# A bidirectional chunked scan and an output projection on TensorE: the order of their matmuls written out by hand

## The chip, the core and the metric

The kernel runs on one core of a Trainium2 chip. The metric is the device time of one execution in microseconds (us), and less is better. TensorE (PE) multiplies matrices into PSUM; VectorE (DVE), ScalarE (ACT) and GpSimd (POOL) do the elementwise work; SyncE (SP) issues every DMA from one queue. The engines run side by side, and each works through its own list of instructions in order.

## The reference

One layer over 17 tiles of 128 tokens (16 of the latent, one of the context). A normalised input is projected to two groups of heads. Group A is a gated linear recurrence, group B a gated DeltaNet; each is scanned forward and backward. The outputs of both are normed per head, gated, joined and multiplied by `w_out`; a SwiGLU feed-forward network (FFN) follows.

```python
def step(s, inp):                 # gated delta rule, one chunk (group B)
    u_c, w_c, attn_c, q_c, kt_c, d_c = inp
    v_new = u_c - jnp.einsum('bhck,bhkv->bhcv', w_c, s)
    o_c = jnp.einsum('bhtk,bhkv->bhtv', q_c, s) + jnp.einsum('bhts,bhsv->bhtv', attn_c, v_new)
    s = s * d_c[..., None, None] + jnp.einsum('bhsk,bhsv->bhkv', kt_c, v_new)
    return s, o_c
...
o_b = ob_f + _flip(ob_b)
o_b = head_rms_norm(o_b, p['gdn_out_norm']) * jax.nn.silu(b_z)
y = jnp.concatenate([o_a, o_b], axis=-1) @ p['w_out']
x = x + g1 * y
h = rms_norm(x, p['norm2']) * (1 + sc2) + sh2
ff = (jax.nn.silu(h @ p['w_gate']) * (h @ p['w_up'])) @ p['w_down']
return x + g2 * ff
```

## The kernel before

The program has three parts: the input projection with group A's recurrence (to about 1297 us), the stage that is changed here (1297 to 1848 us), and the FFN. The stage holds three kinds of work on TensorE.

**The rest of the inverse.** `A3` turns the triangular systems of group B into inverses, one block for each of the 17 chunks, with some ten of them in this stage. A block is 56 float32 matmuls of 32 or 64 columns (lines 675, 681, 686, 696, 701) in a chain PE, ACT, PE, DVE, PE, ACT, PE, DVE, and its triangular solve (`A2`, lines 635 and 637) has run on POOL or DVE before. The last solve is that of the context tile.

**The scan.** `scan(d, c, pre)` does one chunk of one direction, in groups of four matmuls (one per head, float32, 128x128): `pkS` (line 927, keys times state), then four DVE operations that make `vn` (929), `pv` (933), an ACT copy `vv` (935), `pS` (938), four DVE operations that make the new state (943), `po` (947), `pa` (954). `scan_pre` of the next chunk gives `pqk` (905). The next chunk's `pkS` needs the new state. The loop takes 16 pairs: forward chunk i and backward chunk 15-i. From i = 8 on both chunks of a pair have been visited by the other direction, and their sum goes on to the projection.

**The output projection.** Per token tile and group (`part` 0 is A, `part` 1 is B, 34 items) `out_a` norms the heads on ACT, transposes them (`ot`, four matmuls, line 820), gates them and splits them into a high and a low part; `out_b` multiplies these by `w_out` in 24 matmuls of 128x512 (`py`, line 847), whose result DVE takes out of PSUM (851, 855) into a tile of the ring `xt5` of two; `out_c` norms five of the tiles for the FFN (`nt`, line 870). `load_wout` brings the eight row blocks of `w_out` through staging tiles `wor` of the same ring `xt5`. Blocks 0 to 3 are loaded ahead of the scan, 4 to 7 in pairs i = 0 to 3. The parts of blocks 4 to 7 lie in the pool `wb`.

Nothing of this order is written down: the framework's scheduler sorts the instructions of each engine by priority and a timing model when the program is built. The source has eight projection items ahead of the scan, then one or two per pair.

Of the kernel before, what the change touches and what calls it, by code (L numbers as in the profile page):

```python
# [15 lines left out]
P = 128  # L16
# [17 lines left out]
def hybrid_step(ctx: ExitStack, tc, x, vecs, ada1, ada2, bada, win, wgt, alog, dtb, sa, sb, wout, wg, wu, wd, normf,  # L34
# [755 lines left out]
    def out_a(c, part, ob):  # L790
# [35 lines left out]
    def out_b(c, part, oh, ol):  # L826

        xt = wk5.tile([P, D], F32, tag="xt5", name="xt5", bufs=2)
        gm = g1
        if part:  # L830
            x2 = wk5.tile([P, D], F32, tag="x2", name="x2", bufs=2)
            dma(out=xt, in_=xa_d[c])
            if c == NL:
                dma(out=x2, in_=x[LAT:TOK])
                gm = wk6.tile([P, D], F32, tag="h2", name="g1c")
                dma(out=gm, in_=mod_d[1:2, 0:D].broadcast_to([P, D]))
            else:
                for w in range(4):
                    dma(out=x2[32 * w:32 * w + 32], in_=rows_of(x, c, w))
        woh, wol = wos[part]  # L840
        for n in range(2):
            cs = slice(512 * n, 512 * n + 512)
            py = ps5.tile([P, 512], F32, tag="y", name="py", bufs=2)
            t = 0
            for k in range(H):
                for a, b in ((oh, woh), (oh, wol), (ol, woh)):
                    nc.tensor.matmul(out=py, lhsT=a[:, k], rhs=b[:, k, cs], start=t == 0,
                                     stop=t == 3 * H - 1)
                    t += 1
            if part:  # L850
                nc.vector.tensor_tensor(out=xt[:, cs], in0=py, in1=xt[:, cs], op=ALU.add)
                nc.gpsimd.tensor_tensor(out=xt[:, cs], in0=xt[:, cs], in1=gm[:, cs], op=ALU.mult)
                nc.gpsimd.tensor_tensor(out=x2[:, cs], in0=x2[:, cs], in1=xt[:, cs], op=ALU.add)
            else:
                nc.vector.tensor_copy(out=xt[:, cs], in_=py)
        if not part:
            dma(out=xa_d[c], in_=xt)
            return None
        dma(out=x2_d[c], in_=x2)
        return x2  # L860

    def norm_T(c, xt, h2, r, bank):

        nc.scalar.activation(out=xt, in_=xt, func=AF.Copy, scale=r)
        c2 = int(c == NL)
        for i in range(2):
            pt = bank()
            for j in range(H):
                k = H * i + j
                nc.tensor.transpose(pt[:, j], xt[:, k * P:(k + 1) * P], ident)  # L870
            for j in range(H):
                k = H * i + j
                nc.vector.tensor_scalar(out=h2[:, k], in0=pt[:, j], scalar1=m2[:, c2, KD + k:KD + k + 1],
                                        scalar2=m2[:, c2, k:k + 1], op0=ALU.mult, op1=ALU.add)
        dma(out=h2_d[c], in_=h2)

    def out_c(c, x2):
        if c in halves[0][:5]:
            norm_T(c, x2, wk6.tile([P, KD, P], F32, tag="h2", name="h2"), row_norm(x2, wk6),
                   lambda: psn.tile([P, H, P], F32, tag="nt", name="nt"))  # L880
# [16 lines left out]
    def scan_pre(d, c, kT, qT, kn, vn, e, X):  # L897
# [4 lines left out]
        pq = ps2.tile([P, H, P], F32, tag="pre", name="pqk", bufs=1)  # L902
        for h in range(H):
            nc.scalar.activation(out=e[:, h], in_=e[:, h], func=AF.Exp, bias=nG[:, d, c, h:h + 1])
            nc.tensor.matmul(out=pq[:, h], lhsT=kT[:, h], rhs=qT[:, h], start=True, stop=True)
        nc.vector.tensor_tensor(out=e, in0=pq, in1=e, op=ALU.mult)
# [3 lines left out]

    visited = set()
    last = [None]

    def scan(d, c, pre):
        kT, qT, kn, vn, at, X = pre
# [8 lines left out]
        if lat:  # L924
# [3 lines left out]
            for h in range(H):  # L928
                nc.vector.scalar_tensor_tensor(out=vn[:, h], in0=pk[:, h], scalar=nrg[:, d, c, h:h + 1],
                                               in1=vn[:, h], op0=ALU.mult, op1=ALU.add)  # L930
        pv = sc_("pv")
# [3 lines left out]
        nc.scalar.activation(out=vv, in_=pv, func=AF.Copy)  # L935
        pS = sc_("pS")
# [4 lines left out]
        if lat:  # L941
            for h in range(H):
                nc.vector.scalar_tensor_tensor(out=Sn[:, h], in0=So[:, h], scalar=eL[:, d, c, h:h + 1],
                                               in1=pS[:, h], op0=ALU.mult, op1=ALU.add)
            po = sc_("po")
# [6 lines left out]
        pa = sc_("pa")  # L952
        for h in range(H):
            last[0] = nc.tensor.matmul(out=pa[:, h], lhsT=at[:, h], rhs=vv[:, h], start=True, stop=True)
        second = c in visited
        visited.add(c)
        if second or not lat and d == 0:
            t = wk6.tile([P, H, P], F32, tag="ob", name="ob", bufs=3)
        else:
            t = W([P, H, P], "of", 2)  # L960
        if lat:
            for h in range(H):
                nc.scalar.activation(out=t[:, h], in_=po[:, h], func=AF.Copy, scale=eG[:, d, c, h:h + 1])
            nc.vector.tensor_tensor(out=t, in0=pa, in1=t, op=ALU.add)
        else:
            nc.scalar.activation(out=t, in_=pa, func=AF.Copy)
        if not second:
            if lat:
                dma(out=ob_d[c], in_=t)
                return None  # L970
            return t
        of = W([P, H, P], "or", 2)
        dma(out=of, in_=ob_d[c])
        nc.gpsimd.tensor_tensor(out=t, in0=t, in1=of, op=ALU.add)
        return t

    stage = []

    def out_step(item=None):

        stage.insert(0, item and (item[0], item[1], out_a(*item)))
        if len(stage) > 1 and stage[1]:
            c, part, a = stage[1]
            stage[1] = (c, part, out_b(c, part, *a))
        if len(stage) > 2:
            it = stage.pop()
            if it and it[1]:
                out_c(it[0], it[2])

    def scan_ctx():  # L990
        ts = []
        for d in range(2):
            a = scan_load(d, NL)
            scan_pre(d, NL, *a)
            ts.append(scan(d, NL, a))
            visited.discard(NL)
        nc.gpsimd.tensor_tensor(out=ts[0], in0=ts[0], in1=ts[1], op=ALU.add)
        return ts[0]
# [4 lines left out]
    todo = []  # L1003
    for _ in range(8):
        out_step(first.pop(0))
# [3 lines left out]
    pres = [scan_load(0, 0), scan_load(1, NL - 1)]  # L1009
    for d in range(2):  # L1010
        scan_pre(d, (0, NL - 1)[d], *pres[d])
    for i in range(NL):
        nxt = [scan_load(0, i + 1), scan_load(1, NL - 2 - i)] if i < NL - 1 else None
        for d, c in ((0, i), (1, NL - 1 - i)):
            o = scan(d, c, pres[d])
            if nxt:
                with tc.issue_after(getattr(last[0], "ins", last[0])):
                    scan_pre(d, (i + 1, NL - 2 - i)[d], *nxt[d])
            if o is not None:
                todo.append((c, 1, o))  # L1020
        pres = nxt
        if i < H:
            load_wout(H + i)
        if i == 2:
            todo.append((NL, 1, scan_ctx()))
        n = -(-len(first) // (8 - i)) if i < 8 else 2
        for _ in range(n):
            if first:
                out_step(first.pop(0))
# [530 lines left out]
```

## Time and profile before

| | us |
|---|---|
| median of 3 runs | 3359.61 (3348.92 to 3360.17) |
| the profiled execution | 3358.57 |
| its span, first to last instruction | 3356.9 |
| PE busy over the span | 3121.5 (93%) |
| last matmul of the input projection starts | 1297.4 |
| last `py` matmul starts | 1834.7 |
| first matmul of the FFN starts | 1848.4 |

The busy share over the span tells little here: the stage of interest is 551 us of it, and its stretches have different limits. The granted clock of TensorE has two levels, 1.2 and 2.4 GHz; a mean of 1.00 is full speed, and matmuls that take twice as long show the lower level. A float32 matmul leaves two instructions in the rows, so that a group of four is x8 there; a `py` matmul or a transpose leaves one. The rows further down are from this execution.

### The profile page before, as it was taken

The numbers are of one execution on the slowest core, as the hardware profiler recorded it, in microseconds if no ns is written. First come the engines' busy times: TensorE is split into PE (matmuls) and PEld (weight loads), VectorE is DVE, ScalarE is ACT, GpSimd is POOL, SyncE is SP. The second block draws the span as 40 slices with busy tenths as digits, with TensorE's granted clock in tenths as the row PEclk, the third lists the DMA queues.
The fourth block names the chain that finished last, engine by engine and source line by source line (L and its number), as shares of the span: only waits on it lengthen the run. The fifth ranks groups of instructions, "written<-read, shape, count | busy, mean of one in ns | idle before, by whom it ended". The sixth has DMA issues, their size and how long they took to land. (4 is left out here: it accounts for less than half of the span.)

```text
span 3356.9 us, 51604 instructions
## 1 busy us (share of the span) xinstructions
PE 3121.5 (93%) x18550; PEld 2792.2 (83%) x18550; DVE 2089.0 (62%) x4016; ACT 1519.0 (45%) x3233; POOL 1254.8 (37%) x1228
## 2 busy tenths in 40 slices
PE   7899989999999799998897999999999999899998
PEld 4687779999998677877786888888899998799997
DVE  4667744474553764564666777778565677565667
ACT  6455435374464544663764555454422223422222
POOL 1100001021121337413566544554545553544446
PEclk8999999999999988999998999999999999999999
DMA  5235410111114667877784877898656766655564
GB/s 221 72 109 145 116 55 29 53 44 36 53 39 138 172 179 230 265 249 253 240 263 152 304 287 286 298 325 314 223 192 212 240 211 230 228 193 194 184 201 155
DMA packets 331009, 620.12 MB, mean 185 GB/s; under 512 B 77818, under 2 KB 177954, under 8 KB 324354
## 3 DMA queue, kind: packets, MB, share of 16 engines
q1 hardware_dynamic: 330754, 616.83, 56.0%
q8 instruction: 147, 2.41, 0.3%
q14 instruction: 108, 0.88, 0.1%
HBM read 435.22 MB, written 181.51 MB: 184 GB/s over the span
## 5 line engine op out<-in xcount | busy, mean ns | idle before, releaser
L257 PE MATMUL pj<-hh,wh 128*128 128x384 f32 (+2 forms) x1480 | 546.0, 369 | 12.9 <-DVE q L464 6.6
L257 PE MATMUL pj<-hl,wh 128*128 128x384 f32 (+2 forms) x1480 | 545.2, 368 | 0.3 <-POOL hl L231 0.3
L257 PE MATMUL pj<-hh,wl 128*128 128x384 f32 (+2 forms) x1480 | 545.3, 369 | 0.0
L257 PEld LDWEIGHTS pj<-hh,wh 128*128 128x128 f32 (+1 forms) x1480 | 280.4, 189 | 45.5 <-DVE q L464 6.8
L257 PEld LDWEIGHTS pj<-hl,wh 128*128 128x128 f32 (+1 forms) x1480 | 280.1, 189 | 29.9 <-issue 3.1
L257 PEld LDWEIGHTS pj<-hh,wl 128*128 128x128 f32 (+1 forms) x1480 | 280.1, 189 | 28.7 <-issue 3.3
L1476 POOL TENSOR_TENSOR u<-u,g 128x384 f32<-128x384 f32 (+1 forms) x132 | 136.3, 1033 | 292.7 <-DVE u L1217 242.8
L494 POOL TENSOR_SCALAR th<-th,nlbh,lbh 128x384 f32<-128x384 f32 (+1 forms) x40 | 60.5, 1513 | 405.8 <-ACT G L492 401.8
L1371 DVE TENSOR_TENSOR acc<-y,acc 128x512 f32<-128x512 f32 x192 | 131.7, 688 | 64.9 <-PE y L1367 58.0
L1209 PE MATMUL z<-x1h,wp 128*128 128x384 f32 (+1 forms) x528 | 142.8, 334 | 17.6 <-ACT wp L1067 14.2
L1067 ACT ACTIVATE wd<-wdr 128x512 fp32r<-128x512 f32 x146 | 90.0, 627 | 149.4 <-PE y L1367 95.4
L1367 PE MATMUL y<-wd,hid0h 128*128 128x512 f32 x432 | 136.4, 399 | 18.7 <-ACT hid0h L1067 10.0
L1464 ACT ACTIVATE g<-g 128x384 f32<-128x384 f32 (+1 forms) x132 | 66.7, 505 | 191.0 <-DVE g L1217 190.1
L1067 ACT ACTIVATE hid0h<-u 128x384 fp32r<-128x384 f32 (+3 forms) x113 | 53.3, 481 | 217.2 <-POOL u L1476 181.2
L1209 PE MATMUL z<-x6h,wp 128*128 128x384 f32 (+1 forms) x528 | 142.7, 333 | 7.2 <-ACT wp L1067 4.6
L246 DVE TENSOR_TENSOR wl<-raw,wh 128x512 fp32r<-128x512 f32 (+1 forms) x74 | 51.7, 698 | 153.6 <-ACT wh L245 153.5
L1371 DVE TENSOR_TENSOR sum<-y,sum 128x512 f32<-128x512 f32 x144 | 99.3, 690 | 75.8 <-PE y L1367 73.3
L1209 PE MATMUL z<-x4h,wp 128*128 128x384 f32 (+1 forms) x528 | 144.5, 331 | 1.3 <-DMA wp<-wpd 1.3
L1209 PE MATMUL z<-x7h,wp 128*128 128x384 f32 (+1 forms) x528 | 144.3, 332 | 1.0 <-DMA wp<-wpd 1.0
L1068 DVE TENSOR_TENSOR wd<-wdr,wd 128x512 fp32r<-128x512 f32 x146 | 111.9, 775 | 51.5 <-ACT wd L1067 50.6
L1209 PE MATMUL z<-x3h,wp 128*128 128x384 f32 (+1 forms) x528 | 142.6, 328 | 0.0
L1209 PE MATMUL z<-x2h,wp 128*128 128x384 f32 (+1 forms) x528 | 140.5, 328 | 1.4 <-DMA wp<-wpd 1.4
(414 smaller groups left out, 8850.6 us busy)
## 6 DMA issues: line engine op xcount, KB each, us to landing
wp<-wpd SPq DMA_DIRECT2D x308, 512.0 KB
wpd<-wp SPq DMA_DIRECT2D x154, 512.0 KB
ld<-qkvd SPq DMA_DIRECT2D x34, 1024.0 KB
wdr<-in_wd_dram SPq DMA_DIRECT2D x66, 512.0 KB
raw<-in_win_dram SPq DMA_DIRECT2D x72, 256.0 KB
e<-grd SPq DMA_DIRECT2D x68, 256.0 KB
at<-in_ada_dram SPq DMA_DIRECT2D x64, 256.0 KB
wr<-in_wg_dram SPq DMA_DIRECT2D x22, 512.0 KB
```

Of the source, the lines that this page charges most:

```text
L246: nc.vector.tensor_tensor(out=wl[:, ks], in0=raw, in1=wh[:, ks], op=ALU.subtract)
L257: nc.tensor.matmul(out=out, lhsT=a[:, k], rhs=b[:, k], start=t == 0, stop=t == 3 * KD - 1)
L494: nc.gpsimd.tensor_scalar(out=th, in0=th, scalar1=nlbh[:, col:col + 1], scalar2=lbh[:, col:col + 1], op0=ALU.mult, op1=ALU.add)
L1067: nc.scalar.activation(out=wh, in_=raw, func=AF.Copy)
L1068: (e or nc.vector).tensor_tensor(out=wl, in0=raw, in1=wh, op=ALU.subtract)
L1209: nc.tensor.matmul(out=z, lhsT=w_[:, k], rhs=x_[:, k, :N], start=t == 0, stop=t == 3 * HK - 1)
L1367: nc.tensor.matmul(out=py, lhsT=u_[:, j * P:j * P + P], rhs=v_, start=t == 0, stop=t == 2)
L1371: nc.vector.tensor_tensor(out=sums[i, j], in0=py, in1=sums[i, j], op=ALU.add)
L1464: nc.scalar.activation(out=g, in_=g, func=AF.Silu)
L1476: nc.gpsimd.tensor_tensor(out=us[i], in0=us[i], in1=gs[i], op=ALU.mult)
```

## The change

The scan, the projection and the norm are cut into pieces, and TensorE's instructions of the whole part are issued in the order in which the source has them (`tc.manual_schedule` for that engine; the other engines are still sorted by the scheduler). `scan` becomes a generator of five groups per chunk: `pkS`, `pv`, `pS`, `po`, `pa`. A pair's groups are listed with the directions in turn, followed by the two `pqk` groups of the next pair. Twice per pair `out_step` moves a line of five stages on by one (head norms; loads and transposes; the 24 matmuls, as eight pieces of three; the row norm; the transposes of the norm) and hands out pieces, which are issued between the scan's groups. Two steps instead of eight items stand ahead of the scan; then two items per pair throughout. The ring `ob` goes from three to four tiles. The counts of matmuls stay.

In the order listings `ld` is the tile of keys and queries, `S_...` a state, `e` the masked decay, `o_...` and `ob` the head outputs.

TensorE, in the middle of the scan. Before:

```order
L905 MATMUL pqk<-ld 128x128 x4
L927 MATMUL pkS<-S_14181,ld 128x128 x4
L933 MATMUL pv<-ld,XT 128x128 x4
L938 MATMUL pS<-vv,ld 128x128 x4
L947 MATMUL po<-S_14181,ld 128x128 x4
L954 MATMUL pa<-vv,e 128x128 x4
L905 MATMUL pqk<-ld 128x128 x4
```

The changed kernel at about the same pair:

```order
L936 MATMUL pkS<-S_13658,ld 128x128 x4
L855 MATMUL py<-woh,oh 128x512
L855 MATMUL py<-wol,oh 128x512
L855 MATMUL py<-woh,ol 128x512
L855 MATMUL py<-woh,oh 128x512
L855 MATMUL py<-wol,oh 128x512
L855 MATMUL py<-woh,ol 128x512
L936 MATMUL pkS<-S_13671,ld 128x128 x4
L824 MATMUL ot<-ident,o_13681 128x128 x4
L855 MATMUL py<-woh,oh 128x512
L855 MATMUL py<-wol,oh 128x512
L855 MATMUL py<-woh,ol 128x512
```

Before, the groups of one direction follow each other here with nothing between; now `py` pieces and the other direction lie between the groups of each.

TensorE at the last blocks of the inverse (`pl_...`, `pn_...`). Before:

```order
L847 MATMUL py<-woh,ol 128x512
L675 MATMUL pl_10954<-dd,L 32x32 x2
L701 MATMUL pl_10921<-kTa 64x64 x8
L675 MATMUL pl_10954<-dd,L 32x32 x14
L847 MATMUL py<-woh,oh 128x512
L847 MATMUL py<-wol,oh 128x512
L847 MATMUL py<-woh,ol 128x512
L933 MATMUL pv<-ld,XT 128x128 x4
L820 MATMUL ot<-ident,o_13504 128x128 x4
L681 MATMUL pl_10954<-NS,dd 32x32 x16
L686 MATMUL pn_10988<-dd,NS 32x32 x4
L938 MATMUL pS<-vv,ld 128x128 x4
```

The changed kernel:

```order
L696 MATMUL pl_10921<-XT_8657,e 64x64 x8
L686 MATMUL pn_10906<-e,kTa 32x32 x4
L675 MATMUL pl_10954<-dd,L 32x32 x16
L701 MATMUL pl_10921<-kTa 64x64 x8
L681 MATMUL pl_10954<-NS,dd 32x32 x16
L686 MATMUL pn_10988<-dd,NS 32x32 x4
L696 MATMUL pl_11003<-XT_8656,L 64x64 x8
L686 MATMUL pn_10988<-dd,NS 32x32 x4
L701 MATMUL pl_11003<-NS 64x64 x8
L855 MATMUL py<-woh,oh 128x512
L855 MATMUL py<-wol,oh 128x512
L855 MATMUL py<-woh,ol 128x512
```

The last 3.2 blocks stood between projection and scan groups at 240 of 816 `py` matmuls; now they stand in one row, 180 matmuls long, at 72 `py` matmuls, in pair i = 1.

ScalarE at the same place, with `woh` the high part of blocks 4 and 5 of `w_out`. Before:

```order
L806 ACTIVATE jk_14092,sq_14091<-o_14084 128x128
L698 ACTIVATE NS<-pl_11003 128x256
L806 ACTIVATE jk_14092,sq_14091<-o_14084 128x128 x3
L126 ACTIVATE sq_14091<-sq_14091 128x4
L815 ACTIVATE o_14084<-o_14084,sq_14091 128x128 x4
L806 ACTIVATE jk_14284,sq_14283<-o_14276 128x128
L904 ACT_TABLE_LOAD
L904 ACTIVATE e<-e,nG 128x128 x4
L806 ACTIVATE jk_14284,sq_14283<-o_14276 128x128
L787 ACTIVATE woh<-wor,vec 128x1024 x2
L806 ACTIVATE jk_14284,sq_14283<-o_14276 128x128 x2
```

The changed kernel:

```order
L678 ACTIVATE kTa<-pl_10872 128x4x32
L668 ACTIVATE XT_8657<-e 32x8x32 x4
L668 ACTIVATE XT_8656<-dd 32x8x32 x4
L698 ACTIVATE kTa<-pl_10921 128x256
L678 ACTIVATE NS<-pl_10954 128x4x32
L698 ACTIVATE NS<-pl_11003 128x256
L787 ACTIVATE woh<-wor,vec 128x1024 x2
L972 ACTIVATE of<-po,eG 128x128 x4
L826 ACTIVATE oh<-gt_12689 128x512
```

In both, the copies into `woh` of the pool `wb` come right behind the last copy of the inverse (`NS<-pl_11003`). The copies of the inverse stood after those of ten projection items, and now stand after those of three.

The core of the diff:

```diff
...
-    def out_a(c, part, ob):
+    def out_a1(c, part, ob):
...
+        return o4, gt
+
+    def out_a2(o4, gt):
...
+    def out_load(c, part):
         xt = wk5.tile([P, D], F32, tag="xt5", name="xt5", bufs=2)
...
+    def out_b(c, part, oh, ol, xt, x2, gm):
         woh, wol = wos[part]
+        py = [None]
+        def piece(n, k):
             cs = slice(512 * n, 512 * n + 512)
...
+            for t, (a, b) in enumerate(((oh, woh), (oh, wol), (ol, woh))):
+                nc.tensor.matmul(out=py[0], lhsT=a[:, k], rhs=b[:, k, cs], start=k + t == 0, stop=k == H - 1 and t == 2)
...
+        return [lambda n=n, k=k: piece(n, k) for n in range(2) for k in range(H)]
...
+    def out_step():
+        item = first.pop(0) if first else todo.pop(0) if todo else None
+        line.insert(0, item and {"c": item[0], "p": item[1], "a": out_a1(*item)})
+        pieces = []
+        if len(line) > 4:
+            it = line.pop()
...
+        if len(line) > 2 and line[2]:
+            it = line[2]
+            own = out_b(it["c"], it["p"], *it["g"], *it["b"])
+        pieces += own[:2]
+        if len(line) > 1 and line[1]:
...
+            it["b"] = out_load(it["c"], it["p"])
+            pieces.append(lambda it=it: heads(it))
+        return pieces + own[2:]
...
-    for _ in range(8):
-        out_step(first.pop(0))
...
+    with tc.manual_schedule(engines={mybir.EngineType.PE}):
+        for _ in range(2):
+            for f in out_step():
+                f()
...
+        for i in range(NL):
+            cs = (i, NL - 1 - i)
+            gens = [scan(d, cs[d], pres[d]) for d in range(2)]
             nxt = [scan_load(0, i + 1), scan_load(1, NL - 2 - i)] if i < NL - 1 else None
+            groups_ = [lambda g=g: next(g, None) for _ in range(5) for g in gens]
+            if nxt:
+                for d in range(2):
+                    groups_.append(lambda d=d: scan_pq(*nxt[d]))
...
+            if i < H:
+                load_wout(H + i)
+            fill = []
+            for j, g in enumerate(groups_):
+                if j in (0, len(groups_) // 2):
+                    for f in fill:
+                        f()
+                    fill = out_step()
+                    left = len(groups_) // 2 if j == 0 else len(groups_) - j
+                if j == 4 and nxt:
+                    for d in range(2):
+                        scan_pre(d, (i + 1, NL - 2 - i)[d], *nxt[d])
+                g()
+                for _ in range(-(-len(fill) // left)):
+                    fill.pop(0)()
+                left -= 1
+            pres = nxt
+        while todo or first or any(line):
+            for f in out_step():
+                f()
```

## Rows read from the trace of the kernel before

**Rows 1.** Windows over five stretches of the stage; the first line names the columns.
```profile
core 0: us, PE busy (x) PEld busy (x) DVE busy (x) ACT busy (x) POOL busy (x), PEclk, DMA share, GB/s
1297.00:1460.00 163.00, 152.41 (x1696) 131.93 (x1695) 100.30 (x278) 109.76 (x344) 73.61 (x131) 0.92 0.85 274
1460.00:1535.00 75.00, 70.06 (x383) 59.48 (x383) 38.26 (x83) 36.30 (x93) 14.59 (x16) 0.95 0.71 235
1535.00:1640.00 105.00, 85.59 (x607) 80.39 (x605) 54.54 (x152) 55.97 (x158) 46.24 (x46) 0.92 0.71 240
1640.00:1813.00 173.00, 158.84 (x955) 137.64 (x956) 115.44 (x306) 105.41 (x304) 100.83 (x86) 0.95 0.72 230
1813.00:1848.40 35.40, 16.46 (x51) 11.31 (x49) 26.95 (x29) 12.04 (x31) 26.50 (x18) 0.74 0.47 162
```

**Rows 2.** Waits of TensorE in 1813:1850, the longest: sum, count, longest, us.
```profile
PE z L1209 <- ACT wp L1067: 13.4, 1, 13.4
```

**Rows 3.** Groups by line, TensorE, 1297:1850: form, count, busy, mean, idle before.
```profile
...
L847 PE MATMUL py<-woh,oh 128*128 128x512 f32 x272 | 113.5, 417 | 4.6 <-ACT oh L822 4.0 <-DVE xt L855 0.5
...
L938 PE MATMUL pS<-vv,ld 128*128 128x128 f32 x272 | 42.7, 306 | 12.5 <-ACT vv L935 11.6 <-POOL A L637 0.8
...
L820 PE MATMUL ot<-ident,ob 128*128 128x128 f32 x68 | 15.4, 295 | 6.9 <-issue 3.6 <-POOL xt L852 2.2 <-POOL x L853 1.1
...
L675 PE MATMUL pl<-dd,L 32*32 32x32 f32 x160 | 5.1, 203 | 0.0
...
```

**Rows 4.** Timeline, TensorE, part of one chunk: start, length, what, [idle <- releaser].
```profile
...
1701.23 1.06 PE L954 MATMUL pa<-vv,e 128*128 128x128 f32 x8
1702.12 1.06 PE L905 MATMUL pqk<-ld 128*128 128x128 f32 x8
...
1703.25 0.39 PE L847 MATMUL py<-wol,oh 128*128 128x512 f32 x1
1703.48 0.39 PE L847 MATMUL py<-woh,oh 128*128 128x512 f32 x1
...
1713.85 1.91 PE L938 MATMUL pS<-vv,ld 128*128 128x128 f32 x8 [1.99 <-ACT vv L935]
1715.55 1.92 PE L954 MATMUL pa<-vv,e 128*128 128x128 f32 x8
...
```

**Rows 5.** Groups by line, TensorE, 1535:1640.
```profile
...
L938 PE MATMUL pS<-vv,ld 128*128 128x128 f32 x88 | 13.8, 307 | 3.9 <-ACT vv L935 3.9
...
L847 PE MATMUL py<-woh,oh 128*128 128x512 f32 x17 | 6.9, 405 | 0.0
...
```

**Rows 6.** Timeline, TensorE, in that stretch.
```profile
...
1587.12 1.06 PE L927 MATMUL pkS<-S,ld 128*128 128x128 f32 x8
1591.47 2.05 PE L933 MATMUL pv<-ld,XT 128*128 128x128 f32 x8 [3.29 <-DVE ld L929]
...
```

**Rows 7.** Waits of TensorE in 1535:1640 and in 1640:1813, the longest of each.
```profile
PE pv L933 <- DVE ld L929: 6.2, 6, 3.3
...
PE pS L938 <- ACT vv L935: 6.8, 9, 2.9
```

**Rows 8.** Timeline, GpSimd, the end of the last batch's solve.
```profile
...
1376.60 2.06 POOL L639 COPY B<-A 48x1024 f32<-48x1024 f32 x1
...
```

**Rows 9.** Timeline, TensorE, one block of the inverse nearly alone on the engine.
```profile
...
1301.10 1.35 PE L675 MATMUL pl<-dd,L 32*32 32x32 f32 x32
...
1313.38 1.57 PE L701 MATMUL pl<-NS 64*64 64x64 f32 x16 [2.40 <-ACT NS L698]
...
```

**Rows 10.** Window of 20 us with the busiest DMA of the second half; columns as in Rows 1.
```profile
1660.00:1680.00 20.00, 16.77 (x100) 14.51 (x101) 16.92 (x53) 16.18 (x46) 13.96 (x13) 0.91 0.96 316
```

**Rows 11.** Timeline, ScalarE, a table load and what follows it.
```profile
...
1706.40 1.28 ACT L126 ACT_TABLE_LOAD   x1
1707.70 0.21 ACT L126 ACTIVATE sq<-sq 128x4 f32<-128x4 f32 x1
...
```

More of the change, by code (lines that the diff above doesn't have):

```diff
@@ L901, in scan_pre @@
                                 channel_multiplier=-s)
-        pq = ps2.tile([P, H, P], F32, tag="pre", name="pqk", bufs=1)
         for h in range(H):
             nc.scalar.activation(out=e[:, h], in_=e[:, h], func=AF.Exp, bias=nG[:, d, c, h:h + 1])
-            nc.tensor.matmul(out=pq[:, h], lhsT=kT[:, h], rhs=qT[:, h], start=True, stop=True)
-        nc.vector.tensor_tensor(out=e, in0=pq, in1=e, op=ALU.mult)
         for t, f in ((vn, vbs), (kn, ek)):
@@ L909, in scan_pre, with scan_pq @@
                                     .to_broadcast([P, H, P]), op=ALU.mult)
+    def scan_pq(kT, qT, kn, vn, e, X):
+        pq = ps2.tile([P, H, P], F32, tag="pre", name="pqk", bufs=1)
+        for h in range(H):
+            nc.tensor.matmul(out=pq[:, h], lhsT=kT[:, h], rhs=qT[:, h], start=True, stop=True)
+        nc.vector.tensor_tensor(out=e, in0=pq, in1=e, op=ALU.mult)
     visited = set()
-    last = [None]
+    todo = []
     def scan(d, c, pre):
@@ L951, in scan @@
             dma(out=o_sb[d].rearrange("h k v -> k h v"), in_=Sn)
-        pa = sc_("pa")
-        for h in range(H):
-            last[0] = nc.tensor.matmul(out=pa[:, h], lhsT=at[:, h], rhs=vv[:, h], start=True, stop=True)
         second = c in visited
@@ L957, in scan @@
         if second or not lat and d == 0:
-            t = wk6.tile([P, H, P], F32, tag="ob", name="ob", bufs=3)
+            t = wk6.tile([P, H, P], F32, tag="ob", name="ob", bufs=4)
         else:
@@ L963, in scan @@
                 nc.scalar.activation(out=t[:, h], in_=po[:, h], func=AF.Copy, scale=eG[:, d, c, h:h + 1])
+        yield
+        pa = sc_("pa")
+        for h in range(H):
+            nc.tensor.matmul(out=pa[:, h], lhsT=at[:, h], rhs=vv[:, h], start=True, stop=True)
+        if lat:
             nc.vector.tensor_tensor(out=t, in0=pa, in1=t, op=ALU.add)
@@ L966, in scan @@
             nc.scalar.activation(out=t, in_=pa, func=AF.Copy)
[L967 to L998, printed above, removed]
+        if not lat:
+            ctx_o.append(t)
+            if d:
+                nc.gpsimd.tensor_tensor(out=ctx_o[0], in0=ctx_o[0], in1=ctx_o[1], op=ALU.add)
+                todo.append((NL, 1, ctx_o[0]))
+            else:
+                visited.discard(NL)
+        elif not second:
+            dma(out=ob_d[c], in_=t)
+        else:
+            of = W([P, H, P], "or", 2)
+            dma(out=of, in_=ob_d[c])
+            nc.gpsimd.tensor_tensor(out=t, in0=t, in1=of, op=ALU.add)
+            todo.append((c, 1, t))
@@ L1008, in hybrid_step @@
         dma(out=S[d], in_=sb[d].rearrange("h k v -> k h v"))
[L1009 to L1015, printed above, removed]
-            if nxt:
[L1017 to L1029, printed above, removed]
-            elif todo:
-                out_step(todo.pop(0))
```

110 lines of the change are left out of this document (64 added, 46 removed).

## The prediction

> **What bounds the kernel now.** I read the windows first [rows 1]. TensorE is busy for 79 to 94% of every stretch up to 1813 us, and VectorE, ScalarE and GpSimd are each below 73%: they only make it wait. The DMA share is 0.85 in the first stretch and 0.71 to 0.72 later. From the table of times, the stage runs from 1297.7 us to the last `py` at 1835.1 us, 537 us; then TensorE waits 13.4 us for an ACT step whose buffer the last `py` frees [rows 2]. That tail hangs on the last `py` in either kernel, so I leave it as it is.
>
> The question is how much of the 537 us is work. The groups by line give counts, the timeline unit costs at full clock. The three `py` forms have 272 matmuls each [rows 3], one every 0.23 us [rows 4]: 816 × 0.2325 = 190 us. `pS` has 272 instructions, 34 groups [rows 3], and the other scan forms 32 or 34 groups: 200 groups, 0.89 us from one to the next (1701.23 to 1702.12 [rows 4]), 178 us. The head transposes are 34 groups of four; one lies between 0.45 us (half a scan group, since it leaves half the instructions) and 0.9 us (15.4 us busy for 17 groups at mixed clocks [rows 3]); I take 0.53, 18 us. The ten norm groups add 4 us. The first form of line 675 has 160 instructions, 32 per block [rows 3, 9], and its other forms about as many: 9.7 blocks, which I put at 4.2 us each (at the lower clock its first group takes 1.35 and its last 1.57 us for 32 and 16 instructions [rows 9], some 7 us for all 56 matmuls, and half of that is 3.5), 41 us. Work is thus 431 us, and the **loss 537 - 431 = 106 us**, idle time and lower clock together.
>
> Where is it? Idle time plus busy time × (1 - clock) gives 23, 8, 26, 22 and (without the 13.4) 10 us for the five stretches [rows 1], 89 us. The rest is modelled lengths that overlap: in the third stretch, counts give 11 chunks of six groups [rows 5], 59 us, with 51 `py` (12 us) and some transposes, 72 us of 105, so 33 rather than 26 us. The scan has no projection between its groups there. `pv` comes 4.35 us after `pkS`, of which 3.29 us are idle, and then takes 2.05 us instead of 1.06 [rows 6]: the engine waited and came back at the lower of its two levels, 1.2 instead of 2.4 GHz. The fourth stretch has projection work, but `pS` waits 1.99 us for `vv` and the next groups stand 1.70 instead of 0.89 us apart [rows 4]. Such waits sum to 6.2 us in 6 places and 6.8 us in 9 [rows 7].
>
> **The change part by part.** No matmul is added or removed, so the 431 us stay. The order is given by the program, so that it does happen is not in doubt on TensorE; the other engines' lists are sorted again.
>
> *Steady pairs.* One pair is now 12 scan groups, two head transposes and 48 `py`: 10.7 + 1.1 + 11.2 = 23.0 us. Between `pkS` and `pv` of a direction stand nine `py`, the other direction's `pkS` and a transpose group: 0.89 + 2.09 + 0.89 + 0.53 = 4.4 us start to start, against the 4.35 us that VectorE's four operations made it [rows 6]: just covered. Between `pv` and `pS` stand 3.0 us, against 1.99 us of wait [rows 4]. Both waits that made the loss go, as long as ACT and DVE are not late by their own queues. What is late next is those queues: in the fourth stretch 6.1 pairs cost ACT 105 us and DVE 115 us [rows 1], 17 and 19 us a pair, under 23. I leave 1.3 us of loss a pair for pairs 2 to 8 (10 us) and 2 us for pairs 10 to 15 (12 us), where sums, norms and residuals are added. Pair 9 has no projection item ready (the context's and the early ones are done, the sums just begin); in the third stretch a pair lost 33 / 5.5 = 6 us: 6 us.
>
> *The beginning.* Eight items were ahead of the scan, now two. The last blocks of the inverse stand in one row of 180 matmuls after 72 `py`. By the order some 77 us of work stand ahead of them, to 1375 us without loss. The last solve ends at 1378.7 us [rows 8], its result goes through memory (I estimate 10 us), and one block takes 13.85 us nearly alone, 1301.10 to 1314.95 [rows 9]. With two blocks in flight the row ends at about 1410 us, where 90 us of work are done: 22 us lost, with nothing else on TensorE's list to fill them. Before that, pair 0 has the same thin cover as the first 16 us of the stage, which lost 10 us on one block; behind it the copies into `woh` hold item 4 back for some 6 us. Sum 38 us, from 25 (the first stretch loses 23 now) to 55 (blocks one after the other lose 3.2 × 9.65 = 31 in place of 22, with 8 more for a transfer of nearly twice my estimate).
>
> *The end.* After the last `pa` there are 99 `py` rather than 48, work that waits for little. The last stretch loses 10 us now; I take 2, between 0 and 10.
>
> *Transfers.* The loads of the scan and the residual rows are not changed in size. In the fourth stretch 230 GB/s × 173 us = 39.8 MB [rows 1]; in 6.1 pairs of 23 to 25 us that is 260 to 284 GB/s. 316 GB/s is seen for 20 us at a share of 0.96 [rows 10], and 274 GB/s over 163 us [rows 1]. So it fits, with little to spare. The fourth `ob` tile costs no instruction.
>
> Loss after: 38 + 10 + 6 + 12 + 2 = 68 us. Gain 106 - 68 = 38 us. The profiled execution took 3358.6 us (its span 3356.9 and 1.7 around it), 1 us under the median: 3359.6 - 38.6 = **3321 us**.
>
> *A rule that speaks against it.* ScalarE takes 1.30 us from the start of a table load to the start of the function behind it, 1.28 of which are the load [rows 11]. The change has `sqrt` for the norms twice per pair with `exp` between, so up to four loads, 5.2 us of ACT per pair, within the 17 us above. The Trainium skill ("ScalarE: Activation LUTs", section "What ACT_TABLE_LOAD costs") gives 1.28 us and a drain of about 1.38 us for a switch; the load agrees, and the drain is not in this trace. By the page four switches would be an estimated 10.6 us a pair instead of 5.2.
>
> **The rivals.**
>
> 1. *Transfers keep the pace, and the beginning is as thin as it can be.* For: the share is 0.71 and more everywhere, the pairs of the fourth stretch now take 28 us, and their loads are issued a pair ahead only. Against: 316 GB/s [rows 10]. If pairs 10 to 15 stay at 28 us, they lose 30 instead of 12 us; with a beginning of 50 instead of 38 us the gain is 8: 3352 us.
> 2. *Slower: the fixed order holds everything behind one late group.* Before, the scheduler put whatever its timing model held to be ready in front; now a late `vn` or `vv` stops also the `py` and the other direction that stand behind it. For: VectorE has 82% of a pair of 23 us to do, and evacuation of `py` stands in its queue ahead of `vn`; `pkS` to `pv` is covered by 0.05 us only. A wait of 2 us costs these 2 us and 0.8 us on each of the next two groups [rows 4], 3.6 us. Over 14 pairs, with 40 us for beginning and end, it breaks even at (106 - 40) / 14 = 4.7 us a pair, 1.3 such waits; with one per direction, two per pair, it is 40 + 14 × 7.2 = 141 us of loss: 3395 us, and 3378 us with five in three pairs. Against: the nine `py` between them are more than any stretch has now.
> 3. *Hardly any loss.* The beginning as now (25), nothing in steady pairs but 6 for pair 9 and 5 elsewhere, 36 us: 3290 us. For: in 1460 to 1535 us, where `py` lies between groups, idle time and clock lose 8 us of 75 [rows 1], and counted by instructions less. Against: the row of 180.
> 4. *The table loads cost twice what they show.* A `vv` behind a load comes 1.3 us later; for two of them a pair over 13 pairs that is 34 us, of which the spare 1.0 us between `pv` and `pS` takes some: 26 us given back, 3347 us. It is the page's drain, which [rows 11] speak against.
>
> **How the numbers follow.** About 0.5%, 17 us, is what a measurement of this kernel can tell from no change. The forecast, 3300 to 3342 us, gets 0.55; the first rival 0.17, the second 0.15, the third 0.10, the fourth 0.03. Faster by over 0.5% are the forecast and the third, 0.65; within it the first and the fourth, 0.20; slower the second, 0.15. The range has to leave out at most 0.2: from 3288 us (the third's middle, half of it out) to 3380 us (the second's milder part in, 0.11 out). The bounds of the beginning (-13, +17) and of the end (-2, +8) lie in it.
>
> **What would show it.** Right: the last `py` ends at about 1797 us and the 13.4 us wait stays behind it; pairs 2 to 8 are 24 to 25 us long at a granted clock of 0.97 or more; `pv` and `pS` wait under 1 us in most pairs; the blocks of the inverse stand with idle time between 1375 and 1415 us; the DMA share of the second half is 0.8 to 0.9. Wrong by rival 1: shares of 0.95 and waits that end with a DMA. By rival 2: waits of 2 us on `vn` or `vv` in most pairs, clock under 0.95, and VectorE's queue full of other rows at that moment. By rival 4: gaps behind ScalarE's table loads. The forecast is also wrong if the sums of 77 and 90 us of work ahead of the last block don't hold, or if pair 9 is not the only one short of items.

## The result and the profile after

The changed kernel takes 3392.5 us (median of four, 3384.3 to 3398.0), the kernel before 3355.1 us; the ratio is 1.011 with a 95% interval of 1.008 to 1.014. It is **slower by 1.1%**, where 3321 us and a gain of 1% were forecast. Its profiled execution has a span of 3396.1 us, 39 us more than that of before. The last `py` starts at 1878.3 us instead of 1834.7, and the FFN's first matmul at 1891.7 instead of 1848.4. The wait between them is as it was, 13.1 us ([rows 2]: 13.4). All of the time was lost inside the stage: 43 us up to the FFN's first matmul, of which the FFN gave back 4.

The same five stretches as in [rows 1], in the kernel after:

```profile
1297.00:1460.00 163.00, 121.19 (x1458) 107.33 (x1458) 78.12 (x208) 83.18 (x239) 72.46 (x130) 0.73 0.74 231
1460.00:1535.00 75.00, 65.93 (x412) 57.43 (x411) 35.01 (x93) 45.35 (x125) 17.25 (x19) 0.94 0.67 222
1535.00:1640.00 105.00, 97.36 (x637) 85.77 (x636) 54.91 (x153) 56.93 (x167) 21.24 (x24) 1.00 0.66 225
1640.00:1813.00 173.00, 135.89 (x871) 120.02 (x870) 108.44 (x303) 106.69 (x312) 92.99 (x83) 0.93 0.70 231
1813.00:1891.70 78.70, 59.75 (x323) 49.79 (x321) 54.56 (x90) 29.00 (x92) 58.88 (x44) 0.90 0.61 195
```

Read it against [rows 1]. In the third stretch, where TensorE was at 85.6 us of 105 and a clock of 0.92, it is now busy for 97.4 us at a clock of 1.00: what was meant for the steady pairs happened. In the first, 152 us busy became 121 at a clock of 0.73; in the fourth, 159 became 136. The DMA share is lower than before in the first four stretches, so the amount of transfers is not what holds it.

The waits of TensorE in the stage after (sum, count, longest), those over 5 us:

```profile
PE pS L949 <- ACT vv L945: 16.4, 11, 4.0
PE z L1257 <- ACT wp L1115: 13.1, 1, 13.1
PE py L855 <- DVE xt L863: 12.5, 2, 8.2
PE nt L881 <- ACT x L1019: 10.2, 1, 10.2
PE pl L696 <- ACT XT L668: 8.6, 1, 8.6
PE pv L943 <- DVE ld L938: 7.6, 4, 3.5
PE nt L881 <- DVE sq L130: 7.0, 1, 7.0
PE nt L881 <- DVE h L884: 6.7, 3, 3.6
PE pl L696 <- DVE XT L690: 6.4, 4, 4.2
PE py L855 <- DVE xt L859: 5.8, 1, 5.8
```

Three kinds were small before: `py` waiting to be evacuated (`xt`, 0.5 us then), the norm's transposes `nt` (2.7 us then, 24 us in five places now), and the blocks of the inverse `pl` (8.4 us then, 21 now).

To place the loss I count, for each pair of the scan, the matmuls that start between the last `pa` of the pair ahead and its own, take them at the unit costs of the prediction, and subtract that work from the pair's time. Pair 0 is counted from 1298 us, with what stands ahead of it; pair 2 has the context tile in it. Loss in us:

| | pair 0 | 1 | 2 | 3 to 8 | 9 | 10 to 15 | to the last `py` | sum |
|---|---|---|---|---|---|---|---|---|
| before | 19 | 3 | 12 | 27 | 5 | 30 | 11 | 107 |
| forecast | 38 for both | | 10 for 2 to 8 | | 6 | 12 | 2 | 68 |
| after | 31 | 33 | 14 | 15 | 16 | 32 | 8 | 150 |

The 43 us between the first row and the last are those by which the last `py` starts later. Against the kernel before, all of it is lost in pairs 0 and 1 (42 us); the 12 us won in pairs 3 to 8 go again in pairs 9 to 15 (13 us). The last steady pairs lost nothing: 7 and 8 took 23 us each with a loss under 0.5, the 23.0 us of the forecast.

Pair 1 after, on TensorE (start, length, what, [idle <- releaser]), the end of the last block and what follows:

```profile
1429.52 1.57 PE L701 MATMUL pl<-NS 64*64 64x64 f32 x16 [0.62 <-ACT NS L698]
1439.27 0.80 PE L855 MATMUL py<-woh,oh 128*128 128x512 f32 x1 [8.17 <-DVE xt L863]
1439.86 0.63 PE L855 MATMUL py<-wol,oh 128*128 128x512 f32 x1
1440.29 0.63 PE L855 MATMUL py<-woh,ol 128*128 128x512 f32 x1
```

The `py` cannot start because the two PSUM banks are full, and they are full because both tiles of the ring `xt5` are held by row blocks 4 and 5 of `w_out`, whose parts (`woh`, `wol`) wait for the memory of the inverse. On ScalarE and VectorE, before that `py`:

```profile
1434.83 2.19 ACT L787 ACTIVATE woh<-wor,vec 128x1024 fp32r<-128x1024 f32 x2 [5.45 <-DMA xtd<-XT]
```

```profile
1436.01 2.48 DVE L788 SCALAR_TENSOR_TENSOR wol<-wor,vec,woh 128x1024 fp32r<-128x1024 f32 x2 [3.95 <-ACT woh L787]
1438.52 1.29 DVE L863 COPY xt<-py 128x512 f32<-128x512 f32 x2
```

ScalarE waits until the last store of the inverse (`xtd`) has landed, VectorE for ScalarE, and only then is `py` taken out into `xt`. Behind the 8.17 us a `py` takes 0.43 us instead of the 0.23 of [rows 4].

### The profile page after: what moved, and what is told of

It is laid out like the page before. It is cut to its first block, busy times and chain, and to the rows that moved or that the text cites. A ratio compares the mean times of both kernels' runs of the same rounds, so it can differ in the third digit from the quotient of the medians.

```text
span 3396.1 us, 51610 instructions
## 1 busy us (share of the span) xinstructions
PE 3116.4 (92%) x18550; PEld 2789.5 (82%) x18550; DVE 2083.0 (61%) x4016; ACT 1519.7 (45%) x3235; POOL 1254.6 (37%) x1228
## 5 line engine op out<-in xcount | busy, mean ns | idle before, releaser
L855 PE MATMUL py<-woh,oh 128*128 128x512 f32 x272 | 126.4, 465 | 18.3 <-DVE xt L863 12.5
L1257 PE MATMUL z<-x5h,wp 128*128 128x384 f32 (+1 forms) x528 | 142.5, 333 | 0.4 <-DMA wp<-wpd 0.3
```

Source lines behind the costliest of these rows:

```text
L855: nc.tensor.matmul(out=py[0], lhsT=a[:, k], rhs=b[:, k, cs], start=k + t == 0, stop=k == H - 1 and t == 2)
L1257: nc.tensor.matmul(out=z, lhsT=w_[:, k], rhs=x_[:, k, :N], start=t == 0, stop=t == 3 * HK - 1)
```

## Experiments

Times are medians; before was measured beside them at 3351.6 to 3353.6 us. The last three columns are read from the traces: start of the last `pa` of pair 1 and of pair 8, and the time from there to the last `py`. The median of the kernel before moved by 3.5 us between these measurements (3351.6 to 3355.1), so a difference of a few us between two rows says nothing.

| kernel | us | ratio to before, 95% | pair 1 | pair 8 | then to the last `py` |
|---|---|---|---|---|---|
| before | 3355 | | 1399 | 1613 | 222 |
| after | 3392.5 | 1.0110 (1.0080 to 1.0141) | 1447 | 1642 | 236 |
| late loads | 3370.7 | 1.0051 (1.0034 to 1.0068) | 1391 | 1607 | 238 |
| norm transposes last in the half pair | 3386.3 | 1.0105 (1.0088 to 1.0122) | 1436 | 1629 | 236 |
| scheduler's order | 3340.5 | 0.9973 (0.9960 to 0.9986) | 1388 | 1613 | 207 |
| eight items ahead | 3373.5 | 1.0066 (1.0051 to 1.0081) | 1469 | 1628 | 223 |
| scheduler's order, late loads | 3320.6 | 0.9902 (0.9878 to 0.9926) | 1390 | 1594 | 206 |
| the same, eight items ahead, one a pair | 3328.4 | 0.9924 (0.9897 to 0.9951) | 1406 | 1607 | 206 |
| late loads, six stages | 3368.3 | 1.0042 (1.0028 to 1.0055) | 1392 | 1608 | 234 |
| fixed order to pair 8 | 3360.9 | 1.0019 (1.0003 to 1.0034) | 1447 | 1643 | 205 |
| no norm | 3402.9 | 1.0159 (1.0138 to 1.0179) | 1466 | 1661 | 221 |
| no norm, scheduler's order | 3350.6 | 0.9998 (0.9980 to 1.0015) | 1486 | 1632 | 196 |
| before with late loads | 3341.1 | 0.9970 (0.9959 to 0.9982) | 1399 | 1601 | 220 |
| fixed order to pair 8, late loads | 3334.3 | 0.9954 (0.9938 to 0.9970) | 1400 | 1619 | 200 |
| late loads, exps behind `vv` | 3350.8 | 0.9997 (0.9984 to 1.0009) | 1395 | 1600 | 229 |
| scheduler's order, late loads, exps behind `vv` | 3320.8 | 0.9901 (0.9887 to 0.9916) | 1394 | 1599 | 202 |
| exps behind `vv` | 3377.4 | 1.0070 (1.0053 to 1.0087) | 1445 | 1631 | 232 |
| late loads, exps behind `vv`, six stages | 3358.9 | 1.0020 (1.0009 to 1.0031) | 1397 | 1604 | 232 |

### The beginning

**Late loads.** One edit on the changed kernel:

```diff
-            if i < H:
-                load_wout(H + i)
+            if 3 <= i < H + 3:
+                load_wout(H + i - 3)
```

> The changed kernel with one edit: row blocks 4 to 7 of w_out are loaded in pairs 3 to 6 instead of 0 to 3, so that they no longer hold both staging tiles of the projection while the inverse ends. Theory (the loss sits at two places, the beginning and the norm transposes): the two waits of py for the staging tile, 4.3 and 8.2 us, go with the half clock behind them, and the row of 180 matmuls of the inverse spreads out; 15 to 20 us under the changed kernel's 3392, so 3372 to 3377. Rival (the fixed order costs wherever a group is late): the waits move to other groups, 3387 to 3395.

3370.7 us, 22 under the changed kernel. The row of 180 matmuls falls apart into pieces between `py` and scan groups, both waits for `xt` L863 are gone, and pair 1 loses 2 us instead of 33. The first stretch of this kernel:

```profile
1297.00:1460.00 163.00, 134.85 (x1537) 117.84 (x1536) 83.67 (x233) 94.04 (x281) 75.82 (x129) 0.85 0.82 265
```

TensorE is granted 0.85 instead of 0.73. Pair 0 keeps most of its loss (25 us of 31), so that has another cause, which no run isolates. Loading later brings 22 us.

**Eight items ahead**, all else as in the changed kernel:

```diff
-        for _ in range(2):
+        for _ in range(8):
             for f in out_step():
```

> The changed kernel with eight items ahead of the scan, as before, instead of two; all else kept. Theory: the beginning loses what it lost in the kernel before (23 us to 1460 us instead of some 66), but the items run out three pairs earlier and the pairs without py lose some 6 us each: 3365 to 3378. Rival (the fixed order costs wherever a group is late): the beginning stays within 10 us of the changed kernel's, 3385 to 3400.

The time, 3373.5 us, lies in the theory's range, but not as it said. Pairs 0 and 1 together still lose 54 us instead of 64, with 144 `py` more among them: work ahead of the scan does not fill the gaps of the inverse when it stands in a fixed place. Against the theory, the pairs without `py` lost little (7 and 8 took 13 us each for 10.7 us of work, 9 lost 7). Some 13 us of the gain lie behind pair 8 (223 us instead of 236), which the theory had not named.

**The kernel before with late loads** (the same edit there).

> The kernel before with one edit, the row blocks 4 to 7 loaded in pairs 3 to 6. Theory (there eight items ahead cover the beginning, and the pieces of the change are what helps): within 5 us of before, 3348 to 3358. Rival (the late loads alone bring the gain of the scheduled version): 3325 to 3338.

3341.1 us, 10 us under before: neither range. So about half of the 22 us is to be had in the kernel before too. There it comes in pair 2, whose loss falls from 12 to 2 us; the windows from 1399 to 1491 us, before and then with the late loads:

```profile
1399.00:1491.00 92.00, 86.67 (x779) 73.32 (x777) 56.68 (x157) 67.57 (x209) 13.59 (x21) 0.96 0.77 256
```

```profile
1399.00:1491.00 92.00, 92.00 (x819) 78.61 (x818) 58.39 (x161) 66.63 (x206) 15.12 (x20) 1.00 0.79 264
```

The waits that go are one of 3.5 us of `pv` for the load of `XT`, and three others of 0.8 us or less; among them `py` had waited only 0.5 us for `xt`. That the staging tiles held up the kernel before in the same way is therefore not shown.

### Fixed order or scheduler

**Scheduler's order.** The pieces, the five stages and the two items ahead stay; only the fixed order goes:

```diff
-    with tc.manual_schedule(engines={mybir.EngineType.PE}):
+    if True:
```

> The changed kernel with its pieces, its five stages and two items ahead, but TensorE's order left to the scheduler as before. Theory: the stretch from 1535 to 1640 us loses its gain (some 20 us, clock under 0.95 again), the waits of nt go (24 us), and the beginning stays as bad, since it still has two items ahead: 3385 to 3395. Rival (the fixed order is the cost): 3350 to 3360, the time of the kernel before or less.

3340.5 us, under both ranges: 52 us less than the changed kernel (46 by the ratios to before) and 12 us less than before. The theory was wrong in its first point. The stretch from 1535 to 1640 us doesn't lose its gain without the fixed order, it has 102.6 us of busy TensorE at a clock of 0.98. Nor does the beginning stay as bad: pairs 0 to 2 lose 62 us instead of 78. The gaps were not closed by the fixed order but by something else in the change: the pieces, the source order with the directions in turn, the smaller number of items ahead, or the tie of `scan_pre` to `pa`, which the change dropped (below). No run separates these.

**Scheduler's order with late loads.**

> Both edits that helped so far: TensorE's order left to the scheduler, and row blocks 4 to 7 loaded in pairs 3 to 6. Theory (the staging tiles and the fixed order are two separate costs): the gains of 22 and 52 us add up, 3392 - 74 = 3318, within 3312 to 3328. Rival (the scheduler already works round the staging tiles): 3335 to 3345, as with the scheduler alone.

3320.6 us: the gains of 22 and 52 us add up within noise (3318 was worked out). It is the fastest kernel of the study, faster than before by 1.0%. Three stretches of it, the first and third as in [rows 1], and pairs 7 to 9:

```profile
1297.00:1460.00 163.00, 147.42 (x1636) 126.89 (x1635) 96.00 (x261) 101.38 (x326) 73.62 (x126) 0.92 0.84 270
...
1535.00:1640.00 105.00, 100.00 (x730) 91.72 (x729) 69.82 (x187) 65.17 (x201) 55.11 (x55) 1.00 0.82 288
...
1570.00:1605.00 35.00, 33.09 (x284) 32.15 (x284) 25.36 (x78) 22.57 (x67) 18.64 (x20) 1.00 1.02 366
```

Between 1570 and 1605 us there is no `py` at all, only scan groups, those of the two directions side by side, and eight transposes, and TensorE is still busy for 33.1 of 35 us at full clock, where the kernel before had gaps of 3.29 us ([rows 6]).

**The same with eight items ahead and one step per pair up to pair 7.**

> As the run with the scheduler's order and the late loads, with eight items ahead of the scan and one step per pair up to pair 7, two from pair 8. Theory (what is missing at the beginning is work to put between the blocks of the inverse): the loss up to the last block falls by 10 to 20 us more and the pairs without items get one each, 3298 to 3312. Rival (transfers set the beginning, not the cover): 3315 to 3330.

3328.4 us, by the medians 8 us slower than with two items ahead, with runs that overlap; pair 0 loses 22 us instead of 16. More cover did not help. The rival's range holds it, but no run shows that its reason, the transfers, is the cause.

**Fixed order to pair 8, then the scheduler.**

```diff
+            if i == 9:
+                cm.__exit__(None, None, None)
             cs = (i, NL - 1 - i)
```

> The changed kernel with the fixed order for the items ahead and pairs 0 to 8 only; from pair 9 on the scheduler sorts. Theory (the fixed order costs where sums, norms and residuals come in, from pair 9): pairs 9 to 15 fall from 202 to 175 to 182 us and the beginning stays, 3365 to 3372. Rival (the beginning makes it all): 3385 to 3395.

3360.9 us, below the theory's range. To pair 8 the trace is that of the changed kernel (1447 and 1643 us), and the rest takes 205 us instead of 236; pairs 9 to 15 alone take 175, as the theory had it. The fixed order costs 31 us from pair 9 on. The waits of TensorE from 1642 to 1848 us now sum to 2.4 us or less for each kind; the first two and the fourth:

```profile
PE pv L943 <- DVE ld L938: 2.4, 2, 1.7
PE pS L949 <- ACT vv L945: 2.4, 3, 1.7
...
PE nt L881 <- DVE h L884: 2.0, 1, 2.0
```

**The same with late loads.**

> Late loads, fixed order for the items ahead and pairs 0 to 8, scheduler from pair 9 on. Theory (staging tiles and the second half of the fixed order are separate, additive costs, and in pairs 0 to 8 the fixed order is about as good as the scheduler's): 3361 - 22 = 3339, from 3328 to 3342. Rival (the fixed order pays off in the first half once the tiles are free): 3310 to 3320, under the 3321 of the scheduler alone.

3334.3 us (3339 worked out). Against the scheduler alone, 3320.6, the fixed order of the first nine pairs costs another 14 us, where the theory held it to be about as good. So the 72 us between the changed kernel and the fastest are 22 for the late loads (3392.5 to 3370.7), 36 for the fixed order from pair 9 on (3370.7 to 3334.3; 32 without the late loads) and 14 for it up to pair 8.

### What holds TensorE from pair 9 on

The longest wait of the stage, on TensorE:

```profile
1655.95 1.06 PE L959 MATMUL po<-S,ld 128*128 128x128 f32 x8
1667.23 1.09 PE L881 MATMUL nt<-ident,x 128*128 128x128 f32 x4 [10.22 <-ACT x L1019]
1668.11 1.92 PE L959 MATMUL po<-S,ld 128*128 128x128 f32 x8
```

and on ScalarE at that time:

```profile
1654.86 1.28 ACT L908 ACT_TABLE_LOAD   x1
1656.15 1.28 ACT L908 ACTIVATE e<-e,nG 128x128 f32<-128x128 f32 x4
...
1659.67 1.26 ACT L908 ACTIVATE e<-e,nG 128x128 f32<-128x128 f32 x4
...
1661.84 0.63 ACT L747 ACTIVATE jk<-x 128x512 f32<-128x512 f32 x1
...
1665.93 1.15 ACT L1019 ACTIVATE x<-x,sq 128x1024 f32<-128x1024 f32 x1 [1.86 <-DVE sq L131]
```

and on GpSimd, the add that completes the row to be normed:

```profile
1654.65 1.27 POOL L861 TENSOR_TENSOR x<-x,xt 128x512 f32<-128x512 f32 x1
```

The row was complete at 1655.9 us. ScalarE first took two `exp` of the next pair and other rows, and came to it at 1661.84. Meanwhile `po` of the other direction, whose inputs were there, stood behind `nt` and waited 10 us with it.

**Norm transposes last in their half pair** (they stood first):

```diff
-        return pieces + own[2:]
+        nt_ = pieces[:n_nt]
+        return pieces[n_nt:] + own[2:] + nt_
```

> The changed kernel with one edit: the two norm transposes of a step are issued last in their half pair instead of first, some 11 us later in TensorE's order. Theory (beginning and norm transposes): the waits of nt (24 us in 5 places) fall under 6 us and the clock behind them is kept; 20 to 28 us under 3392, so 3364 to 3372. Rival (the fixed order costs wherever a group is late): pS and pv of the same stretch wait instead, 3387 to 3395.

3386.3 us, 6 us less by the medians and 2 by the ratios to before, which is not clear of noise; the theory's range is missed. The time from pair 8 to the last `py` is 236 us, as in the changed kernel.

**Six stages** (the transposes a whole step later, with a third tile `x2` and late loads):

```diff
-        if len(line) > 4:
+        if len(line) > 5:
```

> The fixed order with the late loads of row blocks 4 to 7, and the norm transposes one step later (six stages, with a third tile x2): the order stays fixed. Theory one (single groups stand too early in the fixed order): without the 24 us of nt waits and the clock behind them, 3340 to 3350. Theory two (with a fixed order the next late group holds the rest): nt waits turn into waits of pS, pqk or py, 3360 to 3372, against 3371 with the late loads alone.

3368.3 us against 3370.7, no difference. `nt` still waits 21 us from 1600 us on. Moving the late group in the fixed order doesn't help.

**No norm**, with the fixed order and with the scheduler's:

```diff
-            it["n"] = it["b"][1]
-            nc.scalar.activation(out=it["n"], in_=it["n"], func=AF.Copy, scale=row_norm(it["n"], wk6))
+            dma(out=h2_d[it["c"]].rearrange("p k t -> p (k t)"), in_=it["b"][1])
```

> The changed kernel with the norm of the first five tiles left out (row norm, the ten groups of transposes and their gates; the raw rows are stored in their place), TensorE's order still fixed. It leaves out 4.4 us of TensorE work. Theory (in the second half the fixed order costs by the norm transposes): the 24 us of their waits and the clock behind them go, pairs 9 to the last py fall from 236 to about 202 us, 3392 - 34 = 3358. Rival (any late group takes their place): 3375 to 3388.

> The same part left out with TensorE's order left to the scheduler, beside the 3340 us with the norm. Both theories: there the norm costs no more than its work and some clock, 5 to 10 us, 3330 to 3336. By the theory of the norm transposes the difference between fixed and scheduled order falls from 52 to under 28 us, by the rival it stays above 42.

3402.9 and 3350.6 us, both slower than with the norm. In both the scheduler put most of the inverse ahead of the scan's first groups, and pair 0 takes 141 and 160 us instead of 71 and 59; why is open, so the totals say nothing here. From pair 8 to the last `py`, the norm left out brings 15 us in the fixed order (236 to 221) and 11 us in the scheduler's (207 to 196). The fixed order costs 25 us there without the norm and 29 with it: the theory of the norm transposes falls. `pS` waits instead; from 1600 us on, in the changed kernel and then without the norm:

```profile
PE pS L949 <- ACT vv L945: 5.9, 5, 2.8
```

```profile
PE pS L949 <- ACT vv L945: 17.1, 9, 3.5
```

One such wait in the changed kernel, on TensorE and on ScalarE:

```profile
1779.49 1.05 PE L943 MATMUL pv<-ld,XT 128*128 128x128 f32 x8
...
1785.65 1.16 PE L949 MATMUL pS<-vv,ld 128*128 128x128 f32 x8 [2.82 <-ACT vv L945]
```

```profile
1779.30 0.57 ACT L945 ACTIVATE vv<-pv 128x512 f32<-128x512 f32 x1
1783.84 1.28 ACT L908 ACTIVATE e<-e,nG 128x128 f32<-128x128 f32 x4 [3.98 <-POOL e L905]
1785.03 0.57 ACT L945 ACTIVATE vv<-pv 128x512 f32<-128x512 f32 x1
```

The second `pv` was done at about 1780.5 us and ScalarE was idle, but the next row of its list was an `exp` of the next pair, which waited 3.98 us for GpSimd. `vv`, and with it TensorE, stood behind that. The kernel before issued `scan_pre` after the `pa` of its direction; the change dropped that tie.

**Exps behind `vv`**: the next pair's `scan_pre` may be issued only after the second direction's `vv`. The edit ties GpSimd's rows of `scan_pre` too, not the exps alone.

```diff
-                    for d in range(2):
-                        scan_pre(d, (i + 1, NL - 2 - i)[d], *nxt[d])
+                    with tc.issue_after(getattr(last[0], "ins", last[0])):
+                        for d in range(2):
+                            scan_pre(d, (i + 1, NL - 2 - i)[d], *nxt[d])
```

With late loads and fixed order:

> Fixed order and late loads (3371 us), and the decay masks of the next pair (scan_pre: two exp groups on ScalarE) may be issued only after the copy vv of the second direction. In the changed kernel's trace vv stood behind such an exp, which itself waited 3.98 us for GpSimd. Theory (ScalarE's list, sorted by the scheduler, holds vv behind work of the next pair, and the fixed order makes TensorE wait with it): pS loses most of its 16 us of waits, pairs 9 to 15 fall by 10 to 20 us, 3350 to 3360. Rival (the place of single rows on ScalarE doesn't matter): the exps are late for pqk instead, 3366 to 3376.

3350.8 us against 3370.7. By the trace, 9 us of it lie behind pair 8 (238 us to 229), 7 ahead. The waits of TensorE for `vv` from 1500 us on, with late loads alone and then with this edit, where they stand behind those that remain:

```profile
PE pS L949 <- ACT vv L945: 12.0, 8, 2.8
```

```profile
PE nt L881 <- DVE h L884: 10.6, 4, 4.0
PE nt L881 <- ACT x L1020: 10.0, 1, 10.0
...
PE pS L950 <- ACT vv L946: 0.3, 1, 0.3
```

On the changed kernel alone:

> The changed kernel with this edit alone. Theory: as with the late loads, 10 to 20 us under 3392, 3372 to 3382. Rival: 3386 to 3396.

3377.4 us, 15 less than the changed kernel; here 4 us lie behind pair 8 (236 us to 232) and 11 ahead. As a control, on the fastest version:

> The same edit on the fastest version so far, the scheduler's order with late loads (3321 us). Theory: there TensorE works on something else while vv is late, so little changes, 3314 to 3326. Rival (the exps ahead of vv cost in either order): 3300 to 3312.

3320.8 against 3320.6 us: nothing, though `vv` was late there too, if less. The waits from 1500 us on, without and with the edit:

```profile
PE pS L949 <- ACT vv L945: 6.5, 4, 3.6
```

```profile
PE pS L950 <- ACT vv L946: 1.2, 2, 1.0
```

The edit is worth 15 to 20 us where TensorE's order is fixed and nothing where it is not. With six stages besides:

> Fixed order with late loads, exps behind vv, and the norm transposes one step later (six stages, three tiles x2). Theory (what holds TensorE in pairs 10 to 12 is ScalarE's list, row norms and exps): with both mended the nt waits fall under 10 us, 3335 to 3350. Rival (the norm chain is late whatever stands ahead of it): as with the exps alone, 3350 to 3360.

3358.9 us, 8 us more than without the sixth stage. The wait of `nt` for one row falls from 10.0 to 3.5 us, others take its place (6.0 us for GpSimd's add, 9.1 us for the drain of `nt`). The norm's chain stays late where its transposes have a fixed place; by which of its steps is not settled, and the remaining 30 us between 3350.8 and 3320.6 are not taken apart further.

## Why the prediction was wrong

**The bound and the work: right.** No matmul was added; the losses by pair sum to 150 us, 43 above before's 107, and the span grew by 39. The forecast took 106 for before.

**Steady pairs: right in mechanism and nearly in size.** Pairs 3 to 8 lost 15 us where before lost 27, pairs 7 and 8 nothing, at a clock of 1.00. But the same was to be had without the fixed order, and I ascribed it to `py` between the groups: the scheduled version with late loads runs pairs 7 to 9, without `py`, in 11 to 14 us. `py` between the groups is not needed for it.

**The beginning: the mechanism was right, the size was not.** 38 us were forecast for pairs 0 and 1, with bounds of 25 and 55; they lost 64. The inverse's row ended at 1431 us instead of 1410: it began at about 1402 us and took 29 us for 13.5 us of work, nearly all of it at the lower clock:

```profile
1402.00:1431.00 29.00, 22.52 (x365) 20.62 (x363) 8.91 (x31) 11.93 (x35) 4.34 (x10) 0.55 0.46 152
```

I had counted waiting for the blocks, but no lower clock, and the copies held item 4 for 8.2 us and not 6. Loading later alone was worth 22 us. The 10 us for the solve's way through memory came from no row: in the changed kernel its last copy ends at 1379.0 us and the read of the result is issued only at 1401.1 (what that cost is not shown):

```profile
1377.03 1.93 POOL L639 COPY B<-A 48x1024 f32<-48x1024 f32 x1
```

```profile
1401.09 0.42 SPq L658 DMA_DIRECT2D dd<-xid  x1
```

Pair 2 adds 14 us, where 10 were meant for seven pairs.

**Pairs 9 to 15: the step that failed.** 6 + 12 us were forecast and 48 came. Handing these pairs to the scheduler took back 31 us, with all ahead of them as it was. "What is late next is those queues" was the right place to look, and the conclusion from it was wrong: 17 and 19 us of ScalarE and VectorE in a pair of 23 say that the work fits, and nothing about its order. An engine that has time to spare can still come late, when the next row of its list waits for something else (3.98 us for GpSimd, above). That one cause is worth 4 to 9 us from pair 9 on. The ten norm transposes had no wait in my sum; they waited 24 us, and without them `pS` waited instead. So what the runs show in place of the step is the fixed order as a whole; how the rest of its 31 us divides stays open.

**The end:** 8 us instead of 2; a `py` there waits 5.8 us for `xt`.

**Rival 2** gave 3395 us for two waits in each of 14 pairs, and 3392 came. The number is close, the pattern is another: pairs 3 to 8 had losses of 0 to 5 us, not 7. That the number fits is luck. Its mechanism is shown in part: 31 us by the run that ends the fixed order at pair 8, and 15 to 20 us in the whole stage by the exps; 22 us came with the late loads, and the wait for the staging tiles it didn't name. **Rival 3** needed a beginning that loses 25 us and falls with the 64. The forecast of 3321 us is the time of the scheduled version with late loads, by chance: that one loses 74 us in all, but in other places (20 in pairs 0 and 1, 17 in pair 2).

**Rival 1** falls: in the first four stretches DMA shares went down, and 366 GB/s were moved for 35 us in the fastest version. **Rival 4** falls too: in the changed kernel the function behind a table load starts 1.29 us after the load's start (1654.86 to 1656.15), as in [rows 11], and the drain that the Trainium skill ("ScalarE: Activation LUTs", section "What ACT_TABLE_LOAD costs") adds is not seen there either.

## What to carry to other kernels

Cutting work into pieces and letting independent chains alternate is one thing, and fixing an engine's order is another; measure them apart. Here all of the change but the fixed order was worth some 20 us (3341 to 3321, both with late loads), and the fixed order cost about 50 (3371 to 3321). If one engine's order is written out while the others' are sorted by a model, read the neighbours' lists at each wait and not their busy shares: a row of the next step that isn't ready holds the one that the fixed engine needs. And before a step is moved, look at which ring its tiles come from: two staging tiles that waited for memory stopped the projection, and with it TensorE, for 8.2 us.

## What the runs showed of the hardware beyond that

Two chains of float32 groups in turn kept TensorE at 33.1 of 35 us and a granted clock of 1.00 with hardly any other work (eight transposes); I had reckoned 6 us lost per such pair from the 3.29 us gaps of [rows 6]. In the same 35 us the core's transfers ran at 366 GB/s, above the 316 GB/s of [rows 10], the highest that the prediction had to go by.
